# 53 series of 20 products of zeros ahead of the first stage of a hybrid decoder step

## The chip, the cores and the metric

The kernel runs on one core of a Trainium2 chip. A core has a matrix engine (TensorE, PE in the profile), a vector engine (DVE), a scalar engine (ACT), a general engine (GpSimd, POOL) and an engine that issues transfers (SyncE, SP); each works through its own queue in order, and they wait for one another through semaphores. The matrix engine reads its operands from the on-chip memory SBUF and writes sums to PSUM, which has eight banks of 512 F32 columns per partition. The metric is the device time of one execution in microseconds.

## What is computed

One inference step of one decoder layer, width 1024, for a prompt of 512 tokens and eight samples of 8 tokens, 576 tokens in all. Shortened from the reference:

```python
u = rms(x) * g_pre_mix
z, xbc, dt, q, k, v, ig, fg, og = split(u @ w_in)        # combined input projection
y_ssd = ssd_scan(silu(causal_conv(xbc)), softplus(dt), ...)   # 16 heads
h_ml  = mlstm_scan(q, k, v, ig, log_sigmoid(fg), ...)         # 4 heads
x = x + rms(concat(gated y_ssd, gated h_ml) @ w_out) * g_post_mix
x = x + rms(cross_attention(rms(x) * g_pre_x, memory k, v) @ w_xo) * g_post_x
x = x + rms((silu(u @ w_gate) * (u @ w_up)) @ w_down) * g_post_ffn      # u = rms(x) * g_pre_ffn
```

It also returns the memory's keys and values and the new states of the convolution and of both scans. None of the products of zeros takes part in this.

## The kernel before

Activations lie transposed: 128 features in the partitions, eight such blocks, 576 tokens in the columns. A factor in F32 is split into two parts of the type float32r (F32R): `uh` and `ul` for the activations, `whi` and `wlo` for the weights. A product of matrices is then three products on TensorE for each block of 128 features, high by high, high by low and low by high, which add up in one PSUM bank (`gemm`, L194 to L205). The 576 tokens are taken as 256 + 320 columns (`HALVES`) in most stages and as 288 + 288 in the later ones, so nearly all products are 128 x 128 weights by 256, 288 or 320 columns; a value stage (L814) takes 512.

In `build`, tiles of a pool with a tag share a fixed number of buffers. The PSUM pool behind `MP` has three banks, that behind `GP` three, that behind `BP` two. `SL(1, ...)` is one of the large places in SBUF, in turn used for `qk` (L469) and others; it has 18,432 bytes per partition. Where instructions have no order written out by hand, a planner orders them by a model of the times; inside `tc.manual_schedule(engines={TE.engine})` TensorE's instructions keep the order of the code.

The start, around which the change stands: `wz`, 256 columns of zeros in BF16, is cleared by the vector engine (L299). `NWARM` = 21 products of `wz` by itself go to the bank `ps_warm` (L302); they keep TensorE occupied until the first data come. Then SyncE and ScalarE issue the loads of `par`, of the input `xraw` block by block, and of the first two units of `w_in` in pieces (L303 to L313). For each block, ScalarE makes `uh` (L321) and the vector engine `ul` (L322); pieces of weights are split by L190 and L191. The first stage (L338 to L340) takes, for each of the eight blocks, three products for each of two weight units and both halves: 96 products into four banks `ps_in`. After it comes the third unit (`w2`, through `gemm`), in whose middle the sums of squares of the input (`ssqx`, L263 to L268) are taken over the partitions by small products (`ps_ss`, L227).

Of the kernel before, what the change touches and what calls it, by code (L numbers as in the profile page):

```python
# [11 lines left out]
F32 = mybir.dt.float32  # L12
F32R = mybir.dt.float32r
BF16 = mybir.dt.bfloat16
# [5 lines left out]
P = 128  # L20
# [95 lines left out]
def build(nc, tc, ctx, I, O):  # L116
    V, A, G, S, TE = nc.vector, nc.scalar, nc.gpsimd, nc.sync, nc.tensor
    mm = TE.matmul
# [11 lines left out]
    def SL(slot, name, dt=F32, shape=(P, KT, T)):  # L130

        return big.tile(list(shape), dt, name=name, tag="s%d" % slot, bufs=1)
# [5 lines left out]
    def MP(name="m"):  # L138
        return pa.tile([P, 512], F32, name=name, tag="a")
# [54 lines left out]
    def gemm(ps, units, xh, xl, t0, n, k0=0, k1=None, order=None, late=0):  # L194


        tiles = [(hi[:, j * P:(j + 1) * P], lo[:, j * P:(j + 1) * P]) for hi, lo, nk in units for j in range(nk)]
        order = order or range(len(tiles))
        for i, k in list(enumerate(order))[k0:k1]:
            (wh, wl), ah, al = tiles[k], xh(k, t0, n), xl(k, t0, n)  # L200
            mm(ps, wh, ah, start=i == 0, stop=False)  # L201
            mm(ps, wh, al, start=False, stop=False)  # L202
            for c in range(late) if i == late - 1 else [i] if i >= late else ():
                m = mm(ps, tiles[order[c]][1], xh(order[c], t0, n), start=False, stop=c == len(tiles) - 1)  # L204
        return m  # L205
# [94 lines left out]
    psw = MP("ps_warm")  # L300
    for _ in range(NWARM):
        mm(psw[:, 0:256], wz[:, 0:128], wz, start=True, stop=True, skip_group_check=True)  # L302
    S.dma_start(par, I["par"])  # L303

    wi = [[wp.tile([P, 1024], F32R, name=k, tag=k, bufs=3) for k in ("whi", "wlo")] for _ in range(2)]
# [46 lines left out]
    stop = gemm(ps0[2][1], [(*w2, KT)], U, UL, 256, 320, 0, NSS)  # L352
# [12 lines left out]
    stop = gemm(ps0[3][0], [(*w3, KT)], U, UL, 0, 256)  # L365
# [335 lines left out]
    for g in range(2):  # L701
        for hb in range(2):
            dst = cpad[:, g, 4 * hb:4 * hb + 4, :].rearrange("p b t -> p (b t)")
            src = bc[:, 2 + g, TP + 32 * hb:TP + 32 * hb + 32]
# [4 lines left out]
    for g in range(2):  # L709
        psb = BP("ps_ls")  # L710
        pb3 = psb.rearrange("p (h t) -> p h t", h=8)
        for h in range(8):
            mm(psb[:, h * TS:(h + 1) * TS], sel[:80, 8 * g + h:8 * g + h + 1].to_broadcast([80, P]), cumst[:, TP:T],
               start=h == 0, stop=h == 7, skip_group_check=True)
# [8 lines left out]
        for h in range(8):  # L723
            k, j = h % 2, (8 * g + h) // 2
            mm(psi[64 * k:64 * k + 64, j * TS:(j + 1) * TS], xdts[:, 8 * g + h, :], lm[:, h, :], start=True, stop=True,
               skip_group_check=True)
# [12 lines left out]
    for b in range(4):  # L739
# [3 lines left out]
        for g in range(2):  # L743
            for hb in (1, 0):
                q = 32 * (2 * g + hb)
                mm(psh[q:q + 32, :], cpad[:, g, 4 * hb + b, :],
                   hns[hb][:, 8 * g:8 * g + 8, :].rearrange("p h k -> p (h k)"),
                   start=b == 0, stop=b == 3, skip_group_check=True)
# [116 lines left out]
    def head_norm(num, ex, n4, pool, jk):  # L865

        ss = pool.tile([P, n4], F32, name="hn_ss", tag="hn_ss", bufs=2)
        for c in range(n4):
            A.activation(jk, num[:, c, 0:256], AF.Square, accum_out=ss[:, c:c + 1])
        d = pool.tile([P, n4], F32, name="hn_d", tag="hn_d", bufs=2)  # L870
        den = num[:, :, 256:257].rearrange("p c o -> p (c o)")
        V.scalar_tensor_tensor(d, den, -1.0, den, op0=ALU.mult, op1=ALU.max)
        V.tensor_tensor(d, d, ex, op=ALU.max)
        V.reciprocal(d, d)
        v = pool.tile([P, n4], F32, name="hn_v", tag="hn_v", bufs=2)
        yy = pool.tile([P, n4], F32, name="hn_y", tag="hn_y", bufs=2)
        a = pool.tile([P, n4], F32, name="hn_a", tag="hn_a", bufs=2)
        V.tensor_tensor(v, d, d, op=ALU.mult)
        V.tensor_tensor(v, v, ss, op=ALU.mult)
        V.tensor_scalar(v, v, 1.0 / 256.0, EPS, op0=ALU.mult, op1=ALU.add)  # L880
        G.tensor_tensor(yy, v, C32("nhalf")[:, :n4], op=ALU.pow)
        V.tensor_tensor(a, yy, yy, op=ALU.mult)
        V.scalar_tensor_tensor(a, a, -0.5, v, op0=ALU.mult, op1=ALU.mult)
        V.scalar_tensor_tensor(a, a, 1.5, yy, op0=ALU.add, op1=ALU.mult)
        V.tensor_tensor(a, a, d, op=ALU.mult)
        return a

    for h in range(4):
        q, k = qk[:, h, :], qk[:, 4 + h, :]
# [11 lines left out]
        for c in range(4):  # L901
            mm(pss[:, c * P:(c + 1) * P], k[:, c * P:(c + 1) * P], q[:, c * P:(c + 1) * P], start=True, stop=True,
               skip_group_check=True)
# [8 lines left out]
        for c in range(4):  # L912
# [10 lines left out]
            else:  # L923
# [3 lines left out]
        f = head_norm(num, expnm[:, :, h:h + 1].rearrange("p c o -> p (c o)"), 4, mp_,  # L927
                      mp_.tile([P, 256], F32, name="hn_jk", tag="hn_jk", bufs=1))
# [11 lines left out]
    ms = st2.enter_context(tc.tile_pool(name="mls", bufs=1, side="right", reuse_waits="tile"))  # L940
    psb = BP("ps_ds")
    pb3 = psb[:, 0:256].rearrange("p (h t) -> p h t", h=4)
    for h in range(4):
        mm(psb[:, h * TS:(h + 1) * TS], sel[:68, h:h + 1].to_broadcast([68, P]), sxst[:, TP:T], start=h == 0, stop=h == 3,
           skip_group_check=True)
# [22 lines left out]
    for hb in range(2):  # L968
        r = slice(32 * hb, 32 * hb + 32)
# [5 lines left out]
        for b in range(4):  # L975
# [3 lines left out]
            for h in range(4):  # L979
                mm(psn[32 * h:32 * h + 32, 0:257], qpad[:, h, bb, :], c0[:, h, 0:257], start=False, stop=b == 3,  # L980
                   skip_group_check=True)
# [19 lines left out]
        f = head_norm(num, ex, 1, ms, hn)  # L1001
# [74 lines left out]
    f = SL(5, "f_mix")  # L1076
# [143 lines left out]
    def out2(j, i):  # L1220
        return gemm2([(*weights(("o", j), I["wout"][j, 1], cut=1024), KT)], act(mixm_h), act(mixm_l), o2_evac(j), "ps_o2", [i])
# [30 lines left out]
    m = out2(7, 0)  # L1252
    with tc.issue_after(m.ins):
        rc = rstd_cols([ssq], HCHUNKS[1], "po1", alloc=B0)
    m = out2(6, 0)
# [21 lines left out]
    def mem_key(h, ws=None):  # L1277

        mk = at.tile([P, 2, 2, 256], F32R, name="mk", tag="mk", bufs=1)
        mo = at.tile([P, 2, 256], F32, name="mko", tag="mo", bufs=2)  # L1280
        for kk in range(2):
            ps = GP("ps_mk")[:, 0:256]
            m = gemm(ps, [(*(ws[kk] if ws else split_w(I["wmk"][2 * h + kk])), KT)], mem_act(0), mem_act(1), 0, 256)
            if kk == 0:
                sample_step(m)
            V.tensor_tensor(mo[:, kk, :], ps, rmem_b, op=ALU.mult)
            split(mk[:, 0, kk, :], mk[:, 1, kk, :], mo[:, kk, :], None if ws else G)
        S.dma_start(O["mk"][:, 2 * h:2 * h + 2, :], mo)
        return (mk, m) if ws else mk

    def mem_value(h, ws=None):

        mv = at.tile([P, 2, 2, 256], F32R, name="mv", tag="mv", bufs=1)
        mo = at.tile([P, 2, 256], F32, name="mvo", tag="mo", bufs=2)

        def ev(_, ps):
            for c in range(2):
                A.activation(mo[:, c, :], ps[:, c * 256:(c + 1) * 256], AF.Copy, scale=rmem[0][:, c:c + 1])
            split(mv[:, 0], mv[:, 1], mo)
            S.dma_start(O["mv"][:, :, h * 256:(h + 1) * 256], mo)  # L1300

        m = gemm_tok(I["wmv"][h], mem_act(0), mem_act(1), CHUNKS[:2], ev, units=ws)
        return mv, m
# [6 lines left out]
    def xq(j, i):  # L1310
        return gemm2([(*weights(("xq", j), I["wxq"][j], cut=1024 if i else CUT), KT)], act(u2h), act(u2l), q_evac(j), "ps_xq", [i])
# [130 lines left out]
    mk, m = mem_key(3, wm[:2])  # L1442
    with tc.issue_after(m.ins):
        rc = rstd_cols([ssq], HCHUNKS[0], "po0", alloc=B0)
    mv, m = mem_value(3, wm[2:])
# [10 lines left out]
    m = xq(4, 1)  # L1456
    with tc.issue_after(m.ins):
        rc2[1] = rstd_cols([ssq2], HCHUNKS[1], "p21", alloc=B1)
    m = xq(5, 1)
    with tc.issue_after(m.ins):  # L1460
        rstd_rows(rc2[1][:, 2:3], HCHUNKS[1][2:], rb2, B1)
    m = xq(6, 1)
# [7 lines left out]
    for h in range(3, -1, -1):  # L1470
# [7 lines left out]
        if last:  # L1478
            mv, m = mem_value(h)
# [10 lines left out]
    f = SL(4, "f_xo")  # L1490
# [227 lines left out]
    for n_, (key, p) in enumerate(order):  # L1718
        src = I[{"xo": "wxo", "g": "wgate", "u": "wup"}[key[0]]][key[1]]
# [636 lines left out]
```

## Time and profile before

| | |
|---|---|
| time, median of 2 runs | 1095.58 us (1095.52 to 1095.63) |
| span of the profiled execution | 1095.0 us |
| records of products on TensorE | 8124 |
| transfers | 182.29 MB, mean 166 GB/s |
| granted clock of TensorE, mean over the span | 0.998 |

The page gives the busy time of each engine, the same in 40 slices, and the chain of work that ended last. A record of a product lasts longer than the distance to the next one, since products run one into another; what a stream of products costs is read from their starts, or from the count of products in a stretch. A few of the records can be missing. "PEld" are the loads of weights, which run beside the products. In the groups by form, `128*128 128x288 f32` means 128 rows by 128 weight columns, and 288 moving columns; F32R stands there as f32.

### The profile page before, as it was taken

Reading aid. Unit: us, or ns where it says so; the run is one execution under the profiler, and the core shown is the slowest. Engines: PE = TensorE matmul, PEld = TensorE weight load, DVE = VectorE, ACT = ScalarE, POOL = GpSimd, SP = SyncE. Lnnn points to the kernel's source line nnn. Section 1 sums busy time; section 2 is a strip of 40 time slices with the busy share of each in tenths; the row PEclk is TensorE's granted clock in tenths of the full one; section 3 lists DMA queues with packets and bytes.
Section 4 is the critical chain, followed back from the end, with each engine's and each line's share of the span. In section 5 each row is a group of like instructions: output and inputs, shape, how many; then the busy total and the mean of one; then the engine's idle time right before and its main releaser. Section 6 shows DMA issues by size and latency. Waiting matters only on the chain.

```text
span 1095.0 us, 20715 instructions
## 1 busy us (share of the span) xinstructions
PE 1084.1 (99%) x8124; PEld 1027.5 (94%) x8124; DVE 754.0 (69%) x1507; ACT 611.7 (56%) x1098; POOL 225.8 (21%) x305
## 2 busy tenths in 40 slices
PE   9999999999999999999999999999999999999997
PEld 8999887778999999999988879999999999999997
DVE  6896785658877775558744546676566877787555
ACT  7767632455654555656545445645566566656653
POOL 1332643313213112000144301100011121111000
PEclk9999999999999999999999999999999999999999
DMA  6785635435655349653467775644386687588532
GB/s 204 170 154 127 170 111 174 163 84 177 189 149 146 106 132 312 205 189 102 150 215 271 264 248 163 217 161 109 104 195 142 150 196 173 116 188 186 128 130 88
DMA packets 58967, 182.29 MB, mean 166 GB/s; under 512 B 6605, under 2 KB 11853, under 8 KB 58357
## 3 DMA queue, kind: packets, MB, share of 16 engines
q1 hardware_dynamic: 42740, 138.06, 39.0%
q0 software_dynamic: 15552, 41.95, 19.8%
q8 instruction: 64, 1.05, 0.4%
q10 hardware_dynamic: 576, 0.95, 0.3%
q14 instruction: 35, 0.28, 0.1%
HBM read 160.28 MB, written 20.65 MB: 165 GB/s over the span
## 4 chain that ended last, share of the span: by engine, by line
PE 88%; DVE 5%; ACT 4%; DMA 2%; issue 1%; SPq 0%; POOL 0%; DVEq 0%; ACTq 0%
PE ps_v L814 5%; PE ps_in L202 4%; PE ps_in L201 4%; PE ps_in L204 4%; PE ps_o L202 3%; PE ps_o L204 3%; PE ps_o L201 3%; PE ps_g L1848 3%; PE ps_g L1849 3%; PE ps_g L1850 3%; PE ps_u L1848 3%; PE ps_u L1850 3%; PE ps_u L1849 3%; PE ps_dn L1848 2%; PE ps_dn L1849 2%; PE ps_dn L202 2%
## 5 line engine op out<-in xcount | busy, mean ns | idle before, releaser
L201 PE MATMUL ps_in<-uh,whi 128*128 128x320 f32 (+1 forms) x544 | 164.0, 302 | 0.4 <-DVE cb L450 0.4
L204 PE MATMUL ps_in<-uh,wlo 128*128 128x320 f32 (+1 forms) x544 | 163.2, 300 | 0.0
L202 PE MATMUL ps_in<-ul,whi 128*128 128x320 f32 (+1 forms) x544 | 162.7, 299 | 0.0
L179 ACT CAST whi<-raw 128x1024 fp32r<-128x1024 f32 (+1 forms) x104 | 105.2, 1013 | 96.2 <-PE ps_in L202 26.1
L186 DVE TENSOR_TENSOR wlo<-raw,whi 128x512 fp32r<-128x512 f32 (+1 forms) x96 | 96.6, 1009 | 66.5 <-ACT whi L179 65.8
L201 PEld LDWEIGHTS ps_in<-uh,whi 128*128 128x128 f32 x544 | 103.1, 190 | 3.4 <-issue 1.7
L204 PEld LDWEIGHTS ps_in<-uh,wlo 128*128 128x128 f32 x544 | 103.0, 190 | 1.2 <-issue 0.4
L202 PEld LDWEIGHTS ps_in<-ul,whi 128*128 128x128 f32 x544 | 103.1, 190 | 0.6
L184 POOL DMA_DIRECT2D wlo<-win x32 | 27.9, 871 | 80.1 <-ACT wlo L183 72.0
L1848 PE MATMUL ps_g<-b,whi 128*128 128x288 f32 x144 | 42.5, 295 | 0.0
L1849 PE MATMUL ps_g<-b,whi 128*128 128x288 f32 x144 | 42.4, 295 | 0.0
L1848 PE MATMUL ps_u<-b,whi 128*128 128x288 f32 x144 | 42.4, 295 | 0.0
L1849 PE MATMUL ps_u<-b,whi 128*128 128x288 f32 x144 | 42.4, 295 | 0.0
L1821 ACT CAST whi<-rawx 128x1024 fp32r<-128x1024 f32 (+1 forms) x26 | 25.7, 987 | 27.8 <-PE ps_dn L1849 13.8
L191 DVE TENSOR_TENSOR wlo<-sw,whi 128x1024 fp32r<-128x1024 f32 (+1 forms) x26 | 29.6, 1140 | 14.9 <-ACT whi L190 14.7
L201 PE MATMUL ps_xo<-qh,whi 128*128 128x288 f32 x128 | 38.5, 302 | 0.2 <-ACT whi L179 0.2
L202 PE MATMUL ps_o<-mixs_l,whi 128*128 128x320 f32 (+1 forms) x128 | 38.2, 299 | 0.0
L204 PE MATMUL ps_o<-mixm_h,wlo 128*128 128x256 f32 (+1 forms) x128 | 38.2, 298 | 0.0
L202 PE MATMUL ps_o<-mixm_l,whi 128*128 128x256 f32 (+1 forms) x128 | 37.9, 296 | 0.0
L201 PE MATMUL ps_xq<-u2h,whi 128*128 128x320 f32 (+1 forms) x128 | 37.9, 300 | 0.0
L201 PE MATMUL ps_o<-mixm_h,whi 128*128 128x256 f32 (+1 forms) x128 | 37.9, 296 | 0.0
L204 PE MATMUL ps_xq<-u2h,wlo 128*128 128x320 f32 (+1 forms) x128 | 37.9, 296 | 0.0
(765 smaller groups left out, 3838.9 us busy)
## 6 DMA issues: line engine op xcount, KB each, us to landing
raw<-win SPq DMA_DIRECT2D x35, 512.0 KB, 3.9
raw<-wout SPq DMA_DIRECT2D x17, 512.0 KB, 3.6
raw<-wxq SPq DMA_DIRECT2D x13, 512.0 KB, 3.6
raw<-wgate SPq DMA_DIRECT2D x13, 512.0 KB, 3.5
raw<-wup SPq DMA_DIRECT2D x13, 512.0 KB, 5.3
wlo<-win POOLq DMA_DIRECT2D x24, 256.0 KB, 5.1
kva<-kc SPq DMA_DIRECT2D x12, 512.0 KB, 5.7
kva<-vc SPq DMA_DIRECT2D x12, 512.0 KB, 6.0
```

Source lines behind the costliest of these rows:

```text
L179: casts.append(A.copy(hi[:, :n], raw[:, :n]))
L184: G.dma_start(lo[:, a:b], src[:, a:b], accum_op=ALU.add)
L186: e.tensor_tensor(lo[:, a:b], raw[:, a:b], hi[:, a:b].bitcast(F32), op=ALU.subtract)
L191: (eng or V).tensor_tensor(lo, src, hi.bitcast(F32), op=ALU.subtract)
L201: mm(ps, wh, ah, start=i == 0, stop=False)
L202: mm(ps, wh, al, start=False, stop=False)
L204: m = mm(ps, tiles[order[c]][1], xh(order[c], t0, n), start=False, stop=c == len(tiles) - 1)
L814: mm(ps, a, b, skip_group_check=True, **kw)
L1821: A.copy(s.h3[:, s.all], s.r2[:, s.all])
L1848: mm(ps, wh, b[0][k], start=start and k == 0, stop=False, skip_group_check=True)
L1849: mm(ps, wh, b[1][k], start=False, stop=False, skip_group_check=True)
L1850: m = mm(ps, wl, b[0][k], start=False, stop=k == nk - 1, skip_group_check=True)
```

## The change

Behind the warm-up products a tile `bench` of 4608 columns in F32R is placed in the large place 1 and cleared by the vector engine. 53 series are set out in the list `SEG`; each is 20 products of a part of `bench` (128 columns as weights) by another part of it (`n` moving columns), into a bank `ps_probe`. `m` shifts the start of the moving columns, `w` that of the weights, both counted in elements; from one product to the next the moving start goes on by 576 elements, in a cycle of four, and that of the weights by 128, in a cycle of eight. The other keys: `ws=0` and `ms=0` keep the weights or the moving columns at one place, `one` puts the start flag on each product, `banks=2` changes between two banks, `o` shifts the output in its bank, `two` takes the moving columns in two pieces with a gap, `b` reads the place as BF16, `f` as F32, `r=64` uses 64 rows. Nothing reads the sums. The order of these products on TensorE is that of the code.

```diff
+    bench = SL(1, "bench", F32R, (P, 4608))
+    V.memset(bench.bitcast(F32), 0.0)
+    b16 = bench.bitcast(BF16)
+    SEG = []
+    for p in range(0, 64, 8):
+        SEG.append(dict(n=288, m=p, w=40))
+    for p in (0, 8, 16, 24, 32, 48):
+        SEG.append(dict(n=288, m=40, w=p))
+    for p in (0, 8, 16, 24, 32, 48):
+        SEG.append(dict(n=288, m=0, w=p))
+    for q, w in ((0, 0), (40, 40), (40, 0), (0, 40), (24, 24), (56, 40)):
+        for n in (256, 320, 512):
+            SEG.append(dict(n=n, m=q, w=w))
+    SEG += [dict(n=288, m=40, w=40, ws=0), dict(n=288, m=40, w=40, ms=0), dict(n=288, m=40, w=40, one=1),
+            dict(n=288, m=40, w=40, banks=2), dict(n=288, m=40, w=40, o=8), dict(n=288, m=40, w=40, two=1),
+            dict(n=288, m=40, w=40, b=1), dict(n=512, m=40, w=40, b=1), dict(n=288, m=40, w=40, b=1, ws=0),
+            dict(n=288, m=44, w=40), dict(n=288, m=42, w=40), dict(n=288, m=40, w=44), dict(n=288, m=40, w=42),
+            dict(n=512, m=0, w=0, f=1), dict(n=288, m=0, w=0, r=64)]
+    pq = [MP("ps_probe"), MP("ps_probe")]
+    with tc.manual_schedule(engines={TE.engine}):
+        for sg in SEG:
+            n = sg["n"]
+            src = b16 if sg.get("b") else bench.bitcast(F32) if sg.get("f") else bench
+            for i in range(20):
+                a = sg["m"] + 576 * (i % 4) * sg.get("ms", 1)
+                b = 2432 + sg["w"] + 128 * (i % 8) * sg.get("ws", 1)
+                nr = sg.get("r", P)
+                mv = src[:nr, a:a + n]
+                if sg.get("two"):
+                    mv = src[:nr, a:a + n + 16].rearrange("p (a b) -> p a b", a=2)[:, :, 0:n // 2]
+                po = pq[i % sg.get("banks", 1)][:, sg.get("o", 0):sg.get("o", 0) + n]
+                if sg.get("two"):
+                    po = po.rearrange("p (a b) -> p a b", a=2)
+                mm(po, src[:nr, b:b + P], mv, start=True if sg.get("one") else i < 2, stop=True, skip_group_check=True)
```

## The prediction

> **What bounds the kernel now.** I read the page first (busy times, slices, chain), then the list of waits of TensorE, then stretches of time with their counts of products, then the timeline of the first microseconds.
>
> ```profile
> span 1095.0 us, 20715 instructions
> PE 1084.1 (99%) x8124; PEld 1027.5 (94%) x8124; DVE 754.0 (69%) x1507; ACT 611.7 (56%) x1098; POOL 225.8 (21%) x305
> PE   9999999999999999999999999999999999999997
> PEclk9999999999999999999999999999999999999999
> PE 88%; DVE 5%; ACT 4%; DMA 2%; issue 1%; SPq 0%; POOL 0%; DVEq 0%; ACTq 0%
> ```
>
> TensorE is busy in every slice and carries 88% of the chain. A busy share says little by itself, because a product's record overlaps the next one's; the waits say more:
>
> ```profile
> PE ps_warm L302 <- DVE wz L299: 1.1, 1, 1.1
> PE ps_ss L227 <- DVE ssqx L268: 0.8, 1, 0.8
> PE ps_in L338 <- ACT whi L190: 0.5, 1, 0.5
> PE ps_in L201 <- DVE cb L450: 0.4, 1, 0.4
> PE ps_ct L553 <- ACT r L532: 0.3, 1, 0.3
> PE ps_xo L201 <- ACT whi L179: 0.2, 1, 0.2
> ```
>
> These are all the waits of TensorE in the span, 3.3 us together. Whatever is put into TensorE's queue can therefore hide under at most about 3 us; the rest is added to the end. The execution shown took 1095.0 us from first to last instruction; the median of the runs is 1095.58, so 0.6 us lie around the span, and I leave them there.
>
> **What a product costs.** The cost of a product in a dense stream is the distance between starts, not the duration of its record. Products at full pace, by width, from stretches that hold one form only (product count in brackets):
>
> ```profile
> 5.95:18.70 12.75, 12.75 (x96) 1.00 0.95 317
> 494.00:507.00 13.00, 13.00 (x111) 1.00 0.42 137
> 527.00:537.00 10.00, 10.00 (x70) 1.00 0.70 256
> 800.00:1030.00 230.00, 229.90 (x1736) 1.00 0.75 166
> ```
> ```profile
> 216.25 0.39 PE L814 MATMUL ps_v<-whi,ul 128*128 128x512 f32 x1
> 220.13 0.26 PE L944 MATMUL ps_ds<-sxst,c 68*128 68x64 bf16 x3
> ```
>
> A count takes in the two products that began before the stretch, so I take two off. 288 columns (800 to 1030): 230/1734 = 132.6 ns. 256 columns (494 to 507): 13/109 = 119.3 ns. 320 columns (527 to 537): 10/68 = 147 ns. 512 columns: 17 products start from 216.25 until the next form at 220.13, so 3.88/17 = 228 ns. Between 256 and 320 columns a column adds (147 - 119.3)/64 = 0.433 ns; what is left of each price is about 8 ns (119.3 - 256 x 0.433 = 8.5; 132.6 - 288 x 0.433 = 7.9; 228 - 512 x 0.433 = 6.3). The first row is the first stage: 48 products of 256 and 48 of 320 columns at 12.75/96 = 132.8 ns, which is (119.3 + 147)/2, so this stage holds no idle time that an earlier load could save.
>
> Two more forms are needed:
>
> ```profile
> 126.19 1.02 PE L615 MATMUL ps_h<-xe,btok 128*128 128x512 f32 x2
> 127.04 0.60 PE L607 MATMUL ps_xt<-c,xs 128*128 128x128 f32 x4
> 119.67 0.34 PE L713 MATMUL ps_ls<-cumst,c 80*128 80x64 bf16 x6
> 119.84 0.39 PE L202 MATMUL ps_in<-ul,whi 128*128 128x320 f32 x1
> ```
>
> L615 is one product in plain F32 and leaves two records: 127.04 - 126.19 = 0.85 us for 512 columns. L713 is in BF16: six products of 64 columns in 0.17 us, 29 ns each, of which 64 x 0.433 = 28 are columns. So I take BF16 at its columns plus 1 ns: 126 ns for 288, 223 for 512. Its bounds are the columns alone and the F32R price of the same width (133, 228): 0.4 us over all 60, too little to matter.
>
> **The change part by part.** *The products.* In the built program the 1060 products stand together in TensorE's queue, behind the warm-up products and three of the first stage's. Of the 53 series, 31 are F32R with 288 columns, 6 each with 256, 320 and 512, two BF16 with 288, one BF16 with 512, one F32 with 512.
> - 620 x 132.6 ns = 82.2 us
> - 120 x 119.3 = 14.3; 120 x 147 = 17.6; 120 x 228 = 27.4
> - BF16: 40 x 126 = 5.0; 20 x 223 = 4.5
> - F32: 20 x 0.85 us = 17.0
>
> Sum 168.0 us, all on TensorE. The same weights again, the same moving columns again, a second bank, a start flag on each product, 64 rows instead of 128: I count none of these as cheaper or dearer. Most of the series differ only in where their operands start, and that the trace can show only in part, since in the built program the F32R operands behind the rows above start 32 bytes past a multiple of 64, while about half of the new ones start on a multiple of 64 and four series in between. One row speaks on weights and moving columns that lie in one tile, as they all do here:
>
> ```profile
> L1848 PE MATMUL ps_g<-b,whi 128*128 128x288 f32 x144 | 42.5, 295 | 0.0
> L1848 PE MATMUL ps_g<-u3h 128*128 128x288 f32 x36 | 10.6, 295 | 0.0
> L1849 PEld LDWEIGHTS ps_g<-b,whi 128*128 128x128 f32 x144 | 27.1, 188 | 0.0
> ```
>
> Where both operands come from the one tile u3h, the record is as long (295 ns) as with two tiles. The bounds per F32R product: below, the columns without the 8 ns (980 x 8 = 7.8 us less); above, the weight load, which the trace gives at 188 ns a piece (last row) and which normally runs beside the product before it, laid open in part of the series (a rival below). I take the row that is nearest: no change.
>
> *The zeros and the start.* Ahead of the products the vector engine clears 4608 columns.
>
> ```profile
> 0.84 0.17 DVE L299 MEMSET wz<- 128x128 uint32 x1 [0.84 <-PEq L2348]
> 1.06 4.41 PE L302 MATMUL ps_warm<-wz 128*128 128x256 bf16 x21 [1.06 <-DVE wz L299]
> 5.95 0.39 PE L338 MATMUL ps_in<-uh,whi 128*128 128x256 f32 x1 [0.48 <-ACT whi L190]
> ```
> ```profile
> L958 POOL MEMSET qpad<- 128x1024 f32 x1 | 1.0, 954 | 0.1
> ```
>
> By the POOL memset (954 ns for 1024 columns) it takes 4.3 us, by the short one of wz (0.17 us for 128) 6.1. From 1.0 on it ends between 5.3 and 7.1 us. The products wait for it, and for three products of the first stage that start at 5.95 and end their starts near 6.35. So it costs between 0 and 0.8 us; I take 0.2 (a length of about 5 us, near the POOL row, whose fixed part weighs less). Queued behind it on the vector engine are ghalf, the ul tiles (L322) and the wlo halves (L191); TensorE now wants them 168 us later, so that delay is free. SyncE's and ScalarE's queues get nothing new; POOL's neither.
>
> *What goes.* While the products run, the loads, ul, wlo, the squares and their sums (L268) come to an end. In the built program these do not wait for TensorE, the copies of L361 behind them do. So the wait of ps_ss for ssqx, 0.8 us, goes. After that ScalarE and the vector engine wait for TensorE's results again, and their lead is bounded by three buffers of weights; the waits of L201 for cb (0.4) and of ps_ct (0.3) may go as well, or not. I take 0.3 of these 0.7: -1.1 us, between 0 and -3. What is late next is nothing new: past the first stage the instructions of every engine stand in the built program as before.
>
> *The sum.* 1095.0 + 168.0 + 0.2 - 1.1 = 1262.1 us of span; with 0.6 around it 1262.7, say 1263.
>
> **The rivals.**
> - *The 8 ns go with the start address.* If products whose operands start on a multiple of 64 bytes drop the fixed part, and all do, the sum falls by 7.8 us: 1255. For it: every row above has one and the same start within 64 bytes, so a fixed loss there would look just like this. Against: nothing shows it as a loss of the address, and about half of the series keep the old start, so 4 us is the more likely size. 12%. The Trainium skill (TensorE: Matmul & The Clock Gate, Back-to-back issue gap) gives a warm gap of N/2.4 + 2.5 ns for single products; the rows here lie 10 ns above it at 256 and 288 columns. By that rule the F32R and BF16 products would cost 140.5 us instead of 151.0, and the time would be 1252.
> - *Weight loads laid open.* A weight load (188 ns) fits under the products before it only because loads and products pass side by side (PEld 94% busy beside PE's 99%). If at some distances in one tile, or at starts off the 32-byte grid, they do not, a product costs 188 ns. With a quarter of the 980 F32R products so hit, 245 x 55 ns = 13.5 us more: 1276. Against: the u3h row. 9%.
> - *Zeros keep TensorE slow.* The 21 warm-up products of zeros take 4.41/21 = 210 ns for 256 columns, and later ones 119. If zeros never bring the faster pace, the 168 us double: 1431. Against: after the zeros alone the first stage goes at 132.8 ns from its first products on. 2%.
> - *The other side: the products cost nothing.* Nobody reads ps_probe. If what is never read is dropped before the chip runs it, the time stays 1096, within the measurement. The point that decides is whether the records appear in the trace; in the built program all 1060 stand in TensorE's queue, so 1%. Hiding them is no way there: TensorE's whole waiting is 3.3 us.
>
> **How the numbers follow.** The forecast has 75%, the four rivals 12, 9, 2 and 1; 1% is for what I do not see. The likeliest case by itself is 1258 to 1268: 3 us for the start and the waits, and the 512-wide and 320-wide prices from short stretches. The range takes in the first rival together with the full 3 us of waits (1255 - 1.9 = 1253) and 2 us for prices from short stretches, and reaches up to some three quarters of the second: 1251 to 1273, which leaves out some 10%. One measurement of this kernel can tell 2% from no change, 22 us; every case but the dropped products lies over 14% above, so slower has 0.98, no change 0.01, faster 0.01.
>
> **What would show it.** In the profile of the changed kernel: 1060 products of ps_probe (1080 records, since the F32 series leaves two each) in one run from about 6.3 to 174 us; 20 products of 288 columns from start to start in 2.65 us; no wait of ps_ss for ssqx; first-stage products at 132.8 ns; from there to the end the same length as before but for a microsecond or so. It would be wrong if the series of one width differ by more than a few nanoseconds a product (then address, distance or bank has a price), if the F32 series takes other than 17 us, or if the part behind the products is longer or shorter than before by more than 3 us.

## The result and the profile after

| | before | after |
|---|---|---|
| time, median of 2 runs each | 1095.58 us | 1262.93 us (1262.83 to 1263.03) |
| ratio, 95% interval | | 1.1522 (1.1503 to 1.1541) |
| span of the profiled execution | 1095.0 us | 1261.3 us |

The forecast was 1263, in a range of 1251 to 1273. From the page of the changed kernel, its head, slices and chain, and the copies of the first stage's sums on ScalarE:

```profile
span 1261.3 us, 22880 instructions
PE 1251.6 (99%) x9204; PEld 1177.3 (93%) x9204; DVE 755.8 (60%) x1508; ACT 611.0 (48%) x1098; POOL 225.5 (18%) x305
PE   9999999999999999999999999999999999999997
DVE  6000007967755787785569545466765787787755
ACT  5000017765234565456557444455546756665644
DMA  5000006855443575538753477757346768667742
PE 93%; DVE 2%; ACT 2%; issue 2%; DMA 1%; POOL 0%; DVEq 0%; ACTq 0%; POOLq 0%
L396 ACT COPY xs<-ps_in 128x256 f32<-128x256 f32 (+1 forms) x4 | 1.5, 398 | 163.2 <-PE ps_in L375 163.2
```

TensorE has 9204 - 8124 = 1080 records more and 167.5 us more of busy time. Slices two to six (a slice is 31.5 us) show what the products do to the others: vector engine, ScalarE and transfers stand still. ScalarE had come to the copies of the first stage's sums (L396), and waited 163.2 us there for TensorE's L375. The busy times of these engines are as before, but for the clearing on the vector engine. That is the whole change at a glance: five slices in which TensorE works alone, and then the old kernel.

The edges of the new stretch, from the timelines of TensorE and of the vector engine (start, length, instruction):

```profile
5.34 0.69 PE L373 MATMUL ps_in<-uh,whi 128*128 128x256 f32 x3 [0.29 <-ACT whi L190]
5.87 0.53 PE L337 MATMUL ps_probe<-bench 128*128 128x288 f32 x2
174.38 0.39 PE L374 MATMUL ps_in<-ul,whi 128*128 128x256 f32 x1
```
```profile
1.91 3.90 DVE L305 MEMSET bench<- 128x4608 f32 x1 [0.91 <-issue]
```

The products run from 5.87 to 174.38, 168.5 us. The clearing starts at 1.91, takes 3.90 us and ends at 5.81, just ahead of the first product, which follows the three products of the first stage without a gap. The waits of TensorE in the changed kernel:

```profile
PE ps_warm L302 <- DVE wz L299: 1.1, 1, 1.1
PE ps_in L204 <- DMA wlo<-win: 0.3, 1, 0.3
PE ps_in L373 <- ACT whi L190: 0.3, 1, 0.3
PE ps_xo L201 <- ACT whi L179: 0.2, 1, 0.2
PE ps_ov L1408 <- ACT prh L190: 0.2, 1, 0.2
```

The waits of ps_ss for ssqx, of L201 for cb and of ps_ct are gone; two short ones have come (wlo from its transfer, ps_ov).

By stretches, cut where a series begins (length in us; TensorE's busy time and count of records, in the first three rows also those of the weight loads; granted clock; share and GB/s of the transfers). The counts take in records that began before:

```profile
5.87:59.10 53.23, 53.23 (x401) 53.23 (x402) 1.00 0.23 81
118.61:134.44 15.83, 15.83 (x121) 15.75 (x119) 1.00 0.00 1
154.30:171.56 17.26, 17.26 (x43) 7.41 (x41) 1.00 0.00 0
```
```profile
64.43:69.00 4.57, 4.57 (x23) 1.00 0.00 0
84.16:88.84 4.68, 4.68 (x22) 1.00 0.01 4
134.44:136.90 2.46, 2.46 (x22) 1.00 0.00 0
136.90:141.22 4.32, 4.32 (x22) 1.00 0.00 0
```

The first row is 20 series of 288 columns at 20 different pairs of starts: 53.23/400 = 133.1 ns, against 132.6 in the kernel's own stream. The second is six series with the same weights, the same moving columns, a start flag on each, two banks, a shifted output, two pieces: 15.83/120 = 131.9 ns. The third is the F32 series. Of the next four, the first two are 512 columns at the starts (0,0) and (40,0), the moving one named first: 228 and 234 ns. The last two are BF16 with 288 and 512 columns: 123 and 216 ns. From series to series, all 31 of F32R with 288 columns lie between 2.63 and 2.83 us, and those above 2.69 are three that begin behind a change of stage or type.

### The profile page after: what moved, and what is told of

The parts are those of the page before. It is cut to its first block, busy times and chain, and to the rows that moved or that the text cites. A ratio compares the mean times of both kernels' runs of the same rounds, so it can differ in the third digit from the quotient of the medians.

```text
span 1261.3 us, 22880 instructions
## 1 busy us (share of the span) xinstructions
PE 1251.6 (99%) x9204; PEld 1177.3 (93%) x9204; DVE 755.8 (60%) x1508; ACT 611.0 (48%) x1098; POOL 225.5 (18%) x305
## 4 chain that ended last, share of the span: by engine, by line
PE 93%; DVE 2%; ACT 2%; issue 2%; DMA 1%; POOL 0%; DVEq 0%; ACTq 0%; POOLq 0%
PE ps_probe L337 13%; PE ps_in L202 5%; PE ps_in L201 5%; PE ps_in L204 5%; PE ps_v L849 3%; PE ps_o L202 3%; PE ps_o L204 3%; PE ps_o L201 3%; PE ps_g L1883 3%; PE ps_g L1884 3%; PE ps_g L1885 3%; PE ps_u L1883 3%; PE ps_u L1885 3%; PE ps_u L1884 3%; PE ps_dn L1883 2%; PE ps_dn L1884 2%
## 5 line engine op out<-in xcount | busy, mean ns | idle before, releaser
L337 PE MATMUL ps_probe<-bench 128*128 128x288 f32 (+6 forms) x1080 | 168.6, 318 | 0.0
L201 PE MATMUL ps_in<-uh,whi 128*128 128x320 f32 (+1 forms) x544 | 163.8, 301 | 0.0
L337 PEld LDWEIGHTS ps_probe<-bench 128*128 128x128 f32 (+1 forms) x1020 | 144.2, 188 | 15.0 <-issue 9.8
L201 PEld LDWEIGHTS ps_in<-uh,whi 128*128 128x128 f32 x544 | 103.1, 190 | 2.7 <-issue 1.7
L396 ACT COPY xs<-ps_in 128x256 f32<-128x256 f32 (+1 forms) x4 | 1.5, 398 | 163.2 <-PE ps_in L375 163.2
L201 PE MATMUL ps_xo<-qh,whi 128*128 128x288 f32 x128 | 38.6, 303 | 0.2 <-ACT whi L179 0.2
```

The source lines that it names most:

```text
L337: mm(po, src[:nr, b:b + P], mv, start=True if sg.get("one") else i < 2, stop=True, skip_group_check=True)
```

## The experiments

None of the kernels below leaves out a part of the step. The four of a group ran on one chip beside the kernel before: group one e1 to e4, group two e5 to e8, group three e9 to e12; the kernel before had medians of 1096.03, 1096.21 and 1096.09 us there, single runs between 1094.57 and 1097.75.

### Are the products alone the added time? (e1, e2, e3, e4)

e1, the clearing without products:

```diff
-        for sg in SEG:
+        for sg in SEG[:0]:
```


> No series is left; the 4608 columns are still cleared. Theory (the products alone carry the added time): 1095.6 us, up to 0.7 more, since ul (L357) now stands behind the clearing, which ended at 5.8 us in the changed kernel, while the first ul began at 5.2 before. Rival (part of the 167 us comes from the clearing, the place in SBUF or the changed order of the first stage): 1098 or more. Time outside the span: 0.6 us as before, if the 1.7 us of the changed kernel come from its products' instructions; 1.7 if they come from the clearing.

1094.19 us: 1.8 below the kernel before by the medians, 1.6 by the ratio of the runs (0.9985, 0.9975 to 0.9994). Neither theory nor rival had that. The clearing costs nothing that shows, so the products carry the added time, and more: 1262.93 - 1094.19 = 168.7 us, or 1263.07 - 1094.19 = 168.9 with e4, which ran on the chip of e1; in the trace they take 168.5. But something in this kernel is better than before. Its list of waits is short:

```profile
PE ps_warm L302 <- DVE wz L299: 1.1, 1, 1.1
PE ps_xo L201 <- ACT whi L179: 0.2, 1, 0.2
```

The three waits that the prediction gave to the lead are gone here without any lead. By their starts in the trace, TensorE's products up to about the 620th, the warm-up counted in, stand in another order than before, and so do instructions of the other engines; in the changed kernel this holds only for products up to the 143rd. This is followed up below. The time outside the span is 1.7 to 1.9 us in the runs of e1 and in those of the kernel before beside it.

e2, two series only:

```diff
+        for sg in SEG[:2]:
```


> Only the first two series, 40 products of 288 columns. Theory (each product at 132.6 ns, and any lead of some microseconds takes away the waits for ssqx, cb and ps_ct, 1.5 us): 1095.6 + 5.3 - 1.5 = 1099.4 us, and no wait of ps_ss for ssqx in the list of waits. Rival (the waits go only with the long lead of 168 us): 1100.9, with ps_ss waiting some 0.8 us.

1101.06 us, 5.0 above the kernel before (interval 3.1 to 6.7). ps_ss no longer waits for ssqx, but the interval holds both times, and a later ps_ss now waits 0.7 us for ssqm, which takes part of it back.

e3, 40 products a series:

```diff
-            for i in range(20):
+            for i in range(40):
```


> 40 products a series instead of 20. Theory (products add at their own pace, nothing of them is hidden, no state of the chip changes in a longer run): 168.3 us more than the changed kernel, 1431.2 us; time outside the span 1.7 us or up to 1 more, if it grows with the number of instructions. Rival (the first ones were partly hidden, or zeros slow down later): off by more than 3 us.

1431.79 us, 168.9 above the changed kernel. The price per product neither falls nor rises in a run twice as long. Time outside the span: 1.7 and 2.0 us.

e4, ones in place of zeros:

```diff
-    V.memset(bench.bitcast(F32), 0.0)
+    V.memset(bench.bitcast(F32), 1.0)
```


> The tile holds 1.0 instead of zeros, all else equal. Theory (the pace does not depend on the data): 1262.9 us, series of 288 columns at 2.63 to 2.67 us. Rival (zeros go faster than data): more than 1266, and the pace of the series above that of the kernel's own products, 132.6 ns.

1263.07 us; in its trace the products run from 6.32 to 174.70, 168.4 us against 168.5 with zeros. Zeros are neither cheaper nor slower than ones.

### What the lead gives back (e5, e6, e9 to e12)

e5 and e6, the kernel before with small edits:

```diff
+    with tc.manual_schedule(engines={TE.engine}):
+        pass
```


> The kernel before, with the loop over the series replaced by an empty block of written order: nothing is cleared, no product is added, but the planner breaks off there and puts some 600 instructions of the first 140 us in another order. Theory (the 1.8 us that e1 came out below the kernel before are this other order, not the clearing): 1.5 to 2 us below the kernel before, 1094.2 us where that shows 1096.0. Rival (they come from the clearing, which shifts the vector engine's start): level with the kernel before within 0.5 us.


```diff
-NSS = 5
+NSS = 7
```


> The kernel before with the constant NSS at 7 instead of 5: two more blocks of the third weight unit are multiplied ahead of the small products ps_ss. Theory (TensorE loses 0.8 us by waiting for ssqx, and two blocks, 0.88 us, fill just that): 0.8 us less than the kernel before. Rival (what hangs on ps_ss comes later instead, and gives it back at ps_ct): within 0.3 us of it.

e5 1093.94 us, 2.3 below the kernel before by the medians, 1.6 by the ratio (0.9985, 0.9976 to 0.9994); e6 1093.77 us, 2.4 below (0.998, 0.9971 to 0.9989). So the gain of e1 belongs to the other order, not to the clearing. In e6 the gain is three times what the two moved blocks can give, so neither its theory nor its rival holds; in its trace TensorE's order past the first stage is that of e5, but for the ps_ss, which come six products later as the edit asks. In e1, e5, e6 and e12 the products ps_ct come 13 products later than before and wait for nothing. In e1, e5 and e6 the additions for ssqx (L268) also end at 23.8 to 23.9 us, against 24.9 in the trace of before. The first stage of e6 is in the order of before, so that part of the order is not needed for the gain. Which of the moved instructions brings it was not tried.

e12, both together:

> The kernel before with the empty block of e5 and with NSS = 7 of e6. Theory (both gained by the same means, the planner's other order of the instructions up to 140 us): no more than either, 2.3 us below the kernel before. Rival (the later ps_ss of e6 is a gain of its own): 3 us or more below.

1094.14 us, 2.0 below (0.998, 0.9971 to 0.9989): no more than either, as the theory has it. Its trace has waits of its own: L268 ends only at 25.1 us, ps_ss waits 0.2 us for it even behind seven blocks, and wlo is late twice, 0.6 us in all. So in nearly the same order the squares come at different times in different executions. These three and e1 are below the kernel before by some two thousandths.

e9, the changed kernel again, and e10, its first eight series:

```diff
+        for sg in SEG[:8]:
```


> The changed kernel once more, beside many runs of the kernel before on the same chip. The 1080 records of its products run for 168.5 us in the trace. Theory (of that, 1.5 us come back, since the waits of TensorE in the first 100 us go): 167.0 us above the kernel before. Rival (nothing comes back, and the shorter rest of the profiled run is scatter of the loads): 168.5 above.

> The first eight series alone, 160 products that take 21.4 us in the trace of the changed kernel; every engine's order is that of the changed kernel. Theory (a lead of 21 us is as good as one of 168, the squares and sums of the input need some 24 us): 21.4 - 1.5 = 19.9 us above the kernel before. Rival (nothing comes back): 21.4 above.

e9 1263.11 us, 167.0 above the kernel before, with an interval of 165.1 to 168.6: the theory's value, but 168.5 is not excluded. e10 1117.35 us, 21.3 above (19.1 to 22.1): nearer to the rival. By their times the two are not told apart; the traces say more. e10 has none of the three early waits, but a new one later, which takes part of it back:

```profile
PE ps_dn L201 <- ACT wdh L190: 0.7, 1, 0.7
PE ps_in L204 <- DMA wlo<-win: 0.4, 1, 0.4
```

e11, a lead without the change, 40 more warm-up products:

```diff
-NWARM = 21
+NWARM = 61
```


> The kernel before with 61 warm-up products instead of 21; no tile is added and no place cleared. The 40 more go at 109 ns, so the first stage starts near 9.7 instead of 5.95 us, 3.7 us later. Theory (a lead of TensorE's rivals of 4 us is enough for the wait for ssqx): 2.5 to 3 us above the kernel before, with no wait of ps_ss for ssqx. Rival (the waits hang on the order of the instructions and stay): 3.7 above.

1099.26 us, 3.2 above (2.0 to 3.9), again between the two. TensorE's first product of the first stage starts at 9.38, 3.4 later than before, and ps_ss waits for nothing. The additions for ssqx, before and in e11:

```profile
18.93 5.94 DVE L268 TENSOR_TENSOR ssqx<-ssqx,sq 128x576 f32<-128x576 f32 x7
17.94 5.94 DVE L268 TENSOR_TENSOR ssqx<-ssqx,sq 128x576 f32<-128x576 f32 x7
```

The timelines give the length of the stretch from the first ps_ss to the first ps_h, which no added product enters. Before, then after, then e11:

```profile
23.78 0.31 PE L204 MATMUL ps_in<-uh,wlo 128*128 128x320 f32 x1
24.93 0.49 PE L227 MATMUL ps_ss<-c,ssqx 128*128 128x1 f32 x3 [0.84 <-DVE ssqx L268]
111.79 0.70 PE L615 MATMUL ps_h<-xe,btok 128*128 128x512 f32 x1
```
```profile
191.83 0.31 PE L204 MATMUL ps_in<-uh,wlo 128*128 128x320 f32 x1
191.98 1.17 PE L227 MATMUL ps_ss<-c,ssqx 128*128 128x1 f32 x10
277.50 0.70 PE L650 MATMUL ps_h<-xe,btok 128*128 128x512 f32 x1
```
```profile
27.34 0.84 PE L227 MATMUL ps_ss<-c,ssqx 128*128 128x1 f32 x7
112.87 0.70 PE L615 MATMUL ps_h<-xe,btok 128*128 128x512 f32 x1 [0.15 <-POOL xe L613]
```

86.86 us before, 85.52 after, 85.53 with a lead of 3.4 us; in e2, e3, e4, e7 to e10 it is 85.5 as well. So some microseconds of lead go with the whole of this gain, and 168 give no more. From ps_h to the end the traces differ again, and not by the length of the lead: 983.2 us before, 983.8 after, 984.1 in e11, 984.8 in e2, 985.4 in e10, 986.6 in e7. Nor is e11 a lead and nothing else: by the starts in its trace the planner has put the first stage in another order too, the changed kernel's but for six products. Every run with a lead has this order, so the two were not tried apart. For ssqx the lead is enough by itself: L268 ends at 23.88 in e11, 24.87 before, and ps_ss starts at 27.34.

### What sets the price of a product (e7, e8)

e7 replaces the list: types, weight columns (`c`) and widths.

```diff
+    for c in (128, 64, 32):
+        for n in (64, 128, 192, 256, 288, 512):
+            SEG.append(dict(n=n, m=40, w=40, c=c))
+    for n in (64, 128, 192, 256, 288, 512):
+        SEG.append(dict(n=n, m=40, w=40, b=1))
+    for n in (128, 256, 288):
+        SEG.append(dict(n=n, m=40, w=40, f=1))
...
-                mm(po, src[:nr, b:b + P], mv,
+                cols = sg.get("c", P)
+                mm(po[:cols], src[:nr, b:b + cols], mv,
```


> The list of series is replaced: F32R with 128, 64 and 32 weight columns by 64, 128, 192, 256, 288 and 512 moving columns; BF16 with 128 by the same six; F32 with 128 by 128, 256 and 288. 20 products each. Theory A (an F32R product cannot be shorter than the load of its weights, and the 8 to 12 ns above the columns are what the load leaves over): with 128 weight columns 64, 128 and 192 moving columns all cost about the same, some 105 to 112 ns, and with 64 and 32 weight columns the price falls, at 288 columns to about 123 ns. Theory B (a fixed part of F32R, whatever its weights): 64, 128 and 192 columns at 36, 64 and 92 ns with all three, 288 at 132. BF16 by both: 29, 56, 82, 109, 122.5, 216 ns. F32: 0.22, 0.43 and 0.48 us.

1175.9 us for e7, and 1248.38 for e8 below, one run each; what is read of them stands in their traces. Stretches of e7, one series each:

```profile
6.26:8.41 2.15, 2.15 (x20) 1.00 1.07 378
10.68:12.94 2.26, 2.26 (x23) 1.00 1.10 367
12.94:15.36 2.42, 2.42 (x23) 1.00 0.94 277
15.36:18.00 2.64, 2.64 (x23) 1.00 0.88 336
22.55:23.69 1.14, 1.14 (x22) 1.00 0.00 0
26.70:28.98 2.28, 2.28 (x22) 1.00 0.03 7
28.98:31.58 2.60, 2.60 (x22) 1.00 0.00 0
36.18:36.82 0.64, 0.64 (x21) 1.00 0.00 0
42.08:44.70 2.62, 2.62 (x23) 1.00 0.00 0
49.34:49.93 0.59, 0.59 (x21) 1.00 0.00 0
52.70:54.88 2.18, 2.18 (x22) 1.00 0.04 8
66.11:74.75 8.64, 8.64 (x43) 1.00 0.00 0
```

The first four are F32R with 128 weight columns by 64, 192, 256 and 288 moving columns: 108, 113, 121 and 132 ns a product. Then 64 weight columns by 64, 256 and 288: 57, 114 and 130. Then 32 by 64 and 288: 32 and 131. Then BF16 by 64 and 256: 30 and 109. Last F32 by 256: 432 ns. Each theory is right in one half. For few moving columns the weights set a floor, 108 to 113 ns for 128 of them and 57 for 64 (theory A); with 32 none shows, for 32 ns is near what BF16 takes for 64 moving columns. But at 288 columns the price hardly depends on the weight columns, 130 to 132 ns, while BF16 in the same place takes 123 by the stretch above: the extra 7 to 9 ns belong to F32R and stay when the weights are fewer (theory B). At 256 both have a part: 121 falls to 114 with fewer weight columns, and BF16 takes 109.

e8 replaces the list by 22 pairs of starts, at 256 and 512 columns:

```diff
+    for n in (256, 512):
+        for m, w in ((0, 0), (0, 8), (0, 16), (0, 24), (0, 32), (0, 40), (0, 48), (0, 56),
+                     (8, 0), (8, 8), (16, 0), (16, 16), (24, 0), (24, 24), (32, 0), (32, 32), (40, 0), (40, 40),
+                     (48, 0), (48, 48), (56, 0), (56, 56)):
+            SEG.append(dict(n=n, m=m, w=w))
```


> The list of series is replaced: 22 pairs of starts at 256 and again at 512 columns, F32R. In the changed kernel 512 columns cost 227 ns at the starts (0,0), (40,40), (24,24) and 232 to 234 at (40,0), (0,40). Theory A (the distance between the two starts decides): all seven pairs with equal starts at 227, all others higher and alike for the same distance. Theory B (where the moving columns start within 64 bytes decides): pairs with m = 0, 16, 32, 48 alike and m = 8, 24, 40, 56 alike, whatever w. Either way no pair is off by more than 10 ns.

Four stretches of 512 columns, at the starts (0,0), (8,0), (16,0) and (40,40), and two of 256, at (0,0) and (0,48):

```profile
58.35:62.91 4.56, 4.56 (x22) 1.00 0.00 0
95.50:100.17 4.67, 4.67 (x22) 1.00 0.00 0
104.74:109.32 4.58, 4.58 (x21) 1.00 0.00 0
137.01:141.54 4.53, 4.53 (x21) 1.00 0.00 0
6.29:8.68 2.39, 2.39 (x20) 1.00 1.03 341
20.51:22.78 2.27, 2.27 (x23) 1.00 0.00 0
```

At 512 columns all eight pairs with equal starts take 4.53 to 4.58 us, (16,0) and (0,48) 4.58 to 4.60, the twelve others 4.65 to 4.68: theory A, with the distance taken modulo 64 elements, 256 bytes. At 256 columns the scatter is 2.27 to 2.40 and equal starts are among the dearest. In the whole scan a start is worth at most 7 ns of a product's price.

## Why the prediction was right, point by point

- **The products, 168.0 us.** 168.5 in the trace, and 168.7 and 168.9 as differences of times (e1, e3). The terms, summed over their series: F32R 288 columns 82.6 (forecast 82.2), 256 14.3 (14.3), 320 17.6 (17.6), 512 27.6 (27.4), BF16 9.1 (9.5), F32 17.3 (17.0). Shown: prices read from starts in stretches of one form carry over to a run of 1060 products; the records' lengths (295 ns at 288 columns) would have given more than twice as much.
- **Nothing hides it.** Shown by e3 and by the slices in which the others stand still. The list of waits that the prediction calls complete has none under 0.15 us; the traced gaps that it leaves out add up to 0.5 us, so the bound of about 3 us holds nearly as it stands.
- **The clearing, 0.2 us.** Its end at 5.81 lies ahead of the first product at 5.87. It began at 1.91 instead of 1.0, and its length was 3.90 us, below the bounds of 4.3 to 6.1; the two errors nearly cancel, and the price is none.
- **What goes, 1.1 us.** The span shows more. First stage 0.6 us earlier (5.34 instead of 5.95), the stretch up to ps_ss shorter by 0.85 ((191.98 - 5.34 - 168.51) against (24.93 - 5.95)), from ps_ss to ps_h 1.34 shorter, from ps_h to the end 0.56 longer (1261.3 - 277.5 against 1095.0 - 111.8): together 2.2 us, and 1095.0 + 168.5 - 2.2 = 1261.3. The first of these is scatter of the first loads: the same start is at 6.32 in e3 and 5.25 in e9. The step took the wait for ssqx as certain and cb and ps_ct as doubtful; all three went, in each run with a lead of 3.4 us or more. The term of 1.1 us was too small for another reason as well: the list counts a wait from the end of the record of the product before, 24.93 - (23.78 + 0.31) = 0.84. From start to start ps_ss came 1.15 us behind that product, and 0.15 in the changed kernel, so this wait cost 1.0 us. From the 124th product behind the warm-up to the L201 that waited for cb both kernels have the same products in the same order: from 22.16 to 97.54 before, from 190.22 to 263.26 after, 2.3 us less, where the list gives 1.5 for the three waits. All this is from one execution of before, of some 1096.8 us, above the kernel's medians; by the medians of e9 1.5 us come back. "What is late next is nothing new" failed in small: new waits of 0.2 to 0.7 us come later. The prediction gave these microseconds to the lead; e1 and e5 show that another order gives them without one.
- **0.6 us around the span.** Wrong. In every run of which both are known, the time is 1.7 to 2.0 us above the span. The page shown of before is of another execution than the two times beside it; by the same 1.7 to 2.0 it belongs to a time of some 1096.8 us, an estimate. So outside the span the forecast added 1.1 us too little (0.6 for 1263.03 - 1261.3 = 1.7, the time and the span of one execution), while it put the span 0.8 us too long (1262.1 for 1261.3). The two errors nearly cancel, and the nearness of 1263 to 1262.93 owes something to that: in part it is luck.
- **The rivals.** Start addresses: no F32R series of 288 columns falls to the 124 ns that the prediction's columns alone would give; the lowest are at 131. But the distance of the two starts has a price at 512 columns: four series at 228 to 229 ns, two at 233 to 234. By the prediction's own sign, more than a few ns, address or distance has a price; here it is worth 0.2 us. The part above the columns goes with the type: from 256 to 512 columns BF16 adds (216 - 109)/256 = 0.42 ns a column, so 288 columns are 120 ns; BF16 in the same place has 2 to 3 ns above them, F32R 11 to 13. By the Trainium skill (TensorE: Matmul & The Clock Gate, Back-to-back issue gap), the warm gap of a single product is N/2.4 + 2.5 ns: for BF16 the trace agrees (109 ns at 256 columns), for F32R it does not (117 to 120 in the changed kernel). Weight loads laid open: no series of 288 columns nears 188 ns. Zeros slow: e4 and the stretches exclude it. Dropped products: 1080 records stand in the trace.

## What to carry to other kernels

Work put on the engine that every slice shows busy costs its full length, and the length is the count times the distance of starts in a stretch of the same type and width; addresses, banks and data were worth some 5 per cent of that at most here. A few microseconds of waits near the start are worth reading for themselves: here an empty block that made the planner choose another order took 2.3 us off by the medians, more than the leads gave back by theirs. Before a span and a time are subtracted, make sure that they are of the same execution.

## What the runs showed of the hardware that was not expected

- A product in F32R costs more than one in BF16 at the same place: 131 to 133 against 123 ns at 288 columns, 114 to 121 against 109 at 256 and 227 to 234 against 216 at 512, with 128 weight columns. F32R with few moving columns has a floor that goes with the weight columns: 108 to 113 ns for 128 of them and 57 for 64.
- A product in F32 is two records, each about twice as long as the same columns in BF16: 512 columns 2 x 0.43 us, 256 columns 2 x 0.216.
- The distance between the starts of weights and moving columns, modulo 256 bytes, is worth 4 to 7 ns at 512 columns in F32R: 227 to 229 ns for equal starts, 233 to 234 for most others.
